# Down-projection of a two-layer diffusion backbone: the quarter sums re-signed and made by adding transfers

## The chip, the cores and the metric

The kernel runs on one core of one Trainium2 chip. The metric is the device time of one execution in microseconds (us); a shorter time is better. The engines are named as in the profile: PE is the matrix engine (PEld its weight loads), DVE the vector engine, ACT the scalar engine, POOL the GpSimd engine, SP the engine that issues most transfers (DMAs). An engine works through its own instructions in order and waits on semaphores for the others.

## The reference

Two layers, each with token mixing and a gated feed-forward part. The change is in the feed-forward part of the 1024 latent tokens; the rest is the same in both kernels.

```python
SEQ = 1024; D_MODEL = 1024; D_FF = 2816; DEPTH = 2

def conv_ffn(h, w_up, conv_w, conv_b, w_down):
    u = h @ w_up
    up = jnp.pad(u, ((0, 0), (1, 1), (0, 0)))
    u = up[:, :-2] * conv_w[0] + up[:, 1:-1] * conv_w[1] + up[:, 2:] * conv_w[2] + conv_b
    a, g = jnp.split(u, 2, axis=-1)
    return (a * jax.nn.silu(g)) @ w_down          # (1024 x 2816) @ (2816 x 1024)

# in each layer l, for the latent tokens x1 and the gate g2
ffn = conv_ffn(x1 * (1 + sc2) + sh2, w_up[l], conv_w[l], conv_b[l], w_down[l])
x = layer_norm(ALPHA * x1 + g2 * ffn, ln2_g[l], ln2_b[l])
```

## The kernel before, in words

All inputs are float32. A float32 product is made of three: each operand is split into a high part, a rounded copy that ACT makes (`whi`, line 1336 in the down-projection), and a low part, the rest, `source - high` (`wlo`, line 1337). `mm3` (lines 158 to 160) adds low*high, high*low and high*high into one PSUM bank, each matmul 128x128 by 128x512.

The down-projection multiplies the gated activations A (tokens by hidden channels) by the weights B (hidden by output channels). Both are cut into quarters, A11 to A22 and B11 to B22, and the product takes seven products of quarters in place of eight (Winograd's form). `DOWN` lists them in their order: P1 = A11 B11, P7 = S3 T3, P6 = S2 T2, P4 = A22 T4, P5 = S1 T1, P3 = S4 B22, P2 = A12 B21. S and T are sums and differences of quarters. A product runs over 11 blocks of 128 hidden channels for four tiles of 128 tokens: 11 x 4 x 3 = 132 matmuls. Its operands come in six steps of one block and then five times two; a step of two blocks is a transfer of 128x1024 floats, 512 KB, for either side.

Before the change every operand that is a sum is made on DVE by `tt` (line 1309) from one or two freshly loaded quarters, and two running sums are held in SBUF: X for the weights (T3, then T2 = T3 + B11) and Y for the activations (S3, then S2 = A22 - S3). T4, T1, S1 and S4 are made from X or Y and another load. DVE makes the low part of the activations, POOL that of the weights. All loads are issued by SP (lines 1292 and 1300). So each step of a product waits for its loads, for the sum, for the cast on ACT and for the low part.

`combine` (line 1354 for its adds) takes a product out of its four PSUM banks and adds it into p1, v and u; `post` (1369, 1370) multiplies by the gate and adds to the residual, which `load_resid` has loaded and scaled: `ga` on DVE (line 997) and `ba`, the beta, on POOL (line 998). These run while the next product is under way, a tile per step. The activations come from a scratch in DRAM, `act`, which the up-projection's `gate` writes (line 1242 is its last multiply) just ahead of the down-projection.

The order in which instructions stand on each engine is made when the kernel is built, by a scheduler that takes buffers and dependences into account; on each engine it is then fixed. The rings of buffers (`raw` for weights, two in each of two pools; `araw` for activations, three; high and low parts, three or four) bound how far the splits run ahead of the matmuls.

Of the kernel before, what the change touches and what calls it, by code (L numbers as in the profile page):

```python
# [19 lines left out]
P = 128  # L20
# [25 lines left out]
# how the parts of a layer's token mixing are laced, and which of their instructions go ahead of others  # L46
# [50 lines left out]
def hybrid_backbone_kernel(ctx: ExitStack, tc: tile.TileContext, A: dict, out: bass.AP):  # L97
# [13 lines left out]
    def f32(ap):  # L111
        return ap.bitcast(F32)

# [67 lines left out]
    def columns(pp, specs, eng=None):  # L181
        # parameter rows to one column per 128 of them
# [149 lines left out]
    # ================= token mixing: projections =================  # L332
# [15 lines left out]
    class Stages:  # L348
        # each use of a product runs its later stages after one and two further products
# [186 lines left out]
    # ================= attention =================  # L536
# [122 lines left out]
    # ================= Fourier mixing =================  # L659
# [85 lines left out]
    # ================= gated linear recurrence =================  # L745
    def recurrence(l, S, gp2, gp, psum):
# [57 lines left out]
        def pair_steps(i):  # L804
            # two tiles of tokens, 2 P of them, side by side
# [111 lines left out]
        # a pair of tiles starts when the one before is halfway  # L917
# [55 lines left out]
    # ================= residual update and layer norm =================  # L973
# [50 lines left out]
    # ================= output projection =================  # L1024
# [35 lines left out]
    # ================= gated convolutional feed-forward =================  # L1060
# [24 lines left out]
    def ffn_weights(fp, n, nraw):  # L1085
        # every fourth unit in a place of its own: one more than the common ring holds
# [11 lines left out]
    def conv(l, j, part, o, u):  # L1098
        # u has one token more than o on either side
# [29 lines left out]
    HALF = SEQ // 2  # L1129

# [44 lines left out]
    def up_early(l, j, h, rp, tag, parked):  # L1175
        # what the later tokens alone allow
# [45 lines left out]
    def up_all(l, fp, todo, ws, h, parked, act, bg):  # L1222
# [10 lines left out]
        def gate(j):  # L1233
            for t0 in (HALF, 0):
# [44 lines left out]
    NK = NJ // 2  # L1279
# [4 lines left out]
    def down_operands(l, f1, f2, f3, act):  # L1284
        X, Y = {}, {}
        count = [0, 0]

        def load_w(fw, q, ks):
            count[0] += 1
            t = (fw if count[0] % 2 else wp).tile([P, 1024], F32, tag="raw", bufs=2, name="raw")[:, 0:512 * len(ks)]  # L1290
            k0, c0 = NK * (int(q[1]) - 1) + ks[0], 512 * (int(q[2]) - 1)
            nc.sync.dma_start(out=t.rearrange("p (k c) -> p k c", c=512),
                              in_=A["w_down"][l, k0 * P:(k0 + len(ks)) * P, c0:c0 + 512].rearrange("(k p) c -> p k c", p=P))
            return t

        def load_a(q, ks, eng=None, first=False):
            t = (wp if first else f1[0]).tile([P, 1024], F32, tag="raw" if first else "araw", bufs=2 if first else 3,
                                              name="araw")[:, 0:512 * len(ks)]
            t0, k0 = HALF * (int(q[1]) - 1), NK * (int(q[2]) - 1) + ks[0]
            (eng or nc.sync).dma_start(out=t.rearrange("p (k c) -> p k c", c=512),  # L1300
                              in_=act[k0:k0 + len(ks), :, t0:t0 + HALF].rearrange("k p c -> p k c"))
            return t

        def hold(held, nm, n, size):
            held[n] = (f3[0] if nm == "X" else f2[0]).tile([P, size], F32, tag=f"{nm}{n}", bufs=1, name=nm)
            return held[n]
# [490 lines left out]
```

## Time and profile before

| what | value |
|---|---|
| time, median of three executions | 3447.15 us (3443.57 to 3452.46) |
| span of the profiled execution, first to last instruction | 3438.2 us |
| down-projection of layer 0 | from 1404.4 to 1688.6 us of the span |
| down-projection of layer 1 | from 3136.4 to 3420.6 us of the span |
| matmuls in one down-projection | 7 x 132 = 924 |

The profile gives the span of its own execution and no other total; the median lies 8.95 us above the span, which is taken as what stands around it. The two down-projections were found by the first and the last matmul into the banks `pd` of the latent tokens, and the seven products by every 132nd matmul. A wait is put down to the instruction that ended it; a busy engine counts only while it executes, so that a full window means an engine without a pause.

### The profile page before, as it was taken

Reading aid. Unit: us, or ns where it says so; the run is one execution under the profiler, and the core shown is the slowest. Engines: PE = TensorE matmul, PEld = TensorE weight load, DVE = VectorE, ACT = ScalarE, POOL = GpSimd, SP = SyncE. Lnnn points to the kernel's source line nnn. Section 1 sums busy time; section 2 is a strip of 40 time slices with the busy share of each in tenths; the row PEclk is TensorE's granted clock in tenths of the full one; section 3 lists DMA queues with packets and bytes.
Section 4 is the critical chain, followed back from the end, with each engine's and each line's share of the span. In section 5 each row is a group of like instructions: output and inputs, shape, how many; then the busy total and the mean of one; then the engine's idle time right before and its main releaser. Section 6 shows DMA issues by size and latency. Waiting matters only on the chain.

```text
span 3438.2 us, 55946 instructions
## 1 busy us (share of the span) xinstructions
PE 3118.6 (91%) x20897; PEld 2535.5 (74%) x20897; DVE 2545.4 (74%) x4167; ACT 1547.9 (45%) x3105; POOL 1412.7 (41%) x1138
## 2 busy tenths in 40 slices
PE   6999998989899999887899999998988889998885
PEld 4879976778666777666697888876766668776664
DVE  4614568877798887698766755668877798887888
ACT  4325556664443434333365435655642534444332
POOL 3521105422554444443435351115435645454545
PEclk9999999999999999999999999999989999999998
DMA  7643122127754443655675432122045532225643
GB/s 214 205 149 84 54 90 60 34 57 217 223 180 140 129 130 121 210 197 176 208 213 182 130 103 71 46 89 67 18 132 170 185 110 80 80 74 183 224 161 117
DMA packets 451396, 457.07 MB, mean 133 GB/s; under 512 B 31859, under 2 KB 343604, under 8 KB 451126
## 3 DMA queue, kind: packets, MB, share of 16 engines
q1 hardware_dynamic: 440342, 443.85, 40.9%
q0 software_dynamic: 10784, 9.66, 1.2%
q8 instruction: 165, 2.70, 0.3%
q14 instruction: 105, 0.86, 0.1%
HBM read 358.88 MB, written 94.54 MB: 132 GB/s over the span
## 4 chain that ended last, share of the span: by engine, by line
PE 17%; DVE 14%; issue 7%; POOL 6%; DMA 4%; ACT 2%; SPq 0%; POOLq 0%; DVEq 0%; ACTq 0%
POOL wlo L1216 3%; PE ps_t L602 2%; PE pu L159 2%; PE pu L158 2%; PE pu L160 2%; DVE cv L1105 1%; DVE wlo L1337 1%; PE ps_s L566 1%; DMA araw<-act 1%; PE ps_o L612 1%; PE ps_s L567 1%; PE ps_o L614 1%; PE pws L158 1%; PE pws L159 1%; PE pws L160 1%
## 5 line engine op out<-in xcount | busy, mean ns | idle before, releaser
L1216 POOL TENSOR_TENSOR wlo<-S,whi 128x512 fp32r<-128x512 f32 x176 | 282.5, 1615 | 279.3 <-ACT whi L1215 266.1
L1105 DVE SCALAR_TENSOR_TENSOR cv<-U,cw,cv 128x512 f32<-128x512 f32 x352 | 332.9, 994 | 32.5 <-ACT cv L1102 32.4
L158 PE MATMUL pd<-whi,wlo 128*128 128x512 f32 x616 | 251.4, 419 | 72.7 <-DVE wlo L1337 54.0
L569 DVE TENSOR_REDUCE mx<-ps_s 128x1 f32<-128x512 f32 (+1 forms) x400 | 222.2, 588 | 107.8 <-PE ps_s L567 106.5
L145 POOL TENSOR_TENSOR wlo<-raw,whi 128x1024 fp32r<-128x1024 f32 x69 | 167.4, 2429 | 300.6 <-ACT whi L144 300.6
L608 DVE TENSOR_TENSOR pl<-ps_t,ph 128x512 fp32r<-128x512 f32 x328 | 222.8, 685 | 85.2 <-ACT ph L607 83.0
L602 PE MATMUL ps_t<-ident,p 128*128 128x128 f32 x1312 | 261.9, 283 | 13.1 <-DVE pl L608 7.5
L159 PE MATMUL pd<-wlo,whi 128*128 128x512 f32 x616 | 255.6, 415 | 17.6 <-POOL wlo L1337 17.6
L576 ACT ACTIVATE p<-ps_s,mx 128x512 f32<-128x512 f32 (+1 forms) x400 | 242.7, 615 | 51.8 <-DVE mx L572 42.1
L607 ACT CAST ph<-ps_t 128x512 fp32r<-128x512 f32 x328 | 190.8, 589 | 160.8 <-PE ps_o L614 80.6
L160 PE MATMUL pd<-whi 128*128 128x512 f32 x616 | 252.0, 409 | 0.0
L1102 ACT ACTIVATE cv<-U,cb,cw 128x512 f32<-128x512 f32 x176 | 137.2, 812 | 254.3 <-DVE U L1231 209.6
L158 PE MATMUL pxs<-whi,hlo 128*128 128x256 f32 x752 | 221.6, 295 | 5.7 <-DVE hraw L1504 4.3
L1337 POOL TENSOR_TENSOR wlo<-raw,whi 128x1024 fp32r<-128x1024 f32 (+1 forms) x60 | 156.5, 2616 | 160.2 <-ACT whi L1336 151.0
L159 PE MATMUL pxs<-wlo,hhi 128*128 128x256 f32 x752 | 216.5, 288 | 0.5 <-DVE wlo L145 0.4
L160 PE MATMUL pxs<-whi,hhi 128*128 128x256 f32 x752 | 216.4, 288 | 0.0
L158 PEld LDWEIGHTS pd<-whi,wlo 128*128 128x128 f32 x616 | 122.0, 199 | 114.8 <-DVE wlo L1337 56.1
L612 PE MATMUL ps_o<-pl,V 128*128 128x256 f32 x656 | 200.4, 322 | 6.7 <-DVE pl L608 4.8
L1216 POOL TENSOR_TENSOR wlo<-raw,whi 128x512 fp32r<-128x512 f32 x108 | 149.9, 1395 | 128.0 <-ACT whi L1215 119.1
L556 POOL DMA_DIRECT2D qt<-QT x72 | 40.3, 560 | 373.9 <-PE ps_s L567 277.1
L602 PEld LDWEIGHTS ps_t<-ident,p 128*128 128x128 f32 x1312 | 164.2, 143 | 36.5 <-DVE pl L608 12.3
L1231 DVE TENSOR_TENSOR U<-pu,U 128x512 f32<-128x512 f32 x252 | 167.3, 685 | 25.5 <-PE pu L160 17.2
(395 smaller groups left out, 9680.2 us busy)
## 6 DMA issues: line engine op xcount, KB each, us to landing
raw<-in_w_up_dram SPq DMA_DIRECT2D x144, 512.0 KB
raw<-in_w_down_dram SPq DMA_DIRECT2D x102, 512.0 KB
raw<-in_w_ada_dram SPq DMA_DIRECT2D x96, 512.0 KB
araw<-act SPq DMA_DIRECT2D x80, 512.0 KB
act<-cv SPq DMA_DIRECT2D x88, 256.0 KB
raw<-in_w_in_dram SPq DMA_DIRECT2D x36, 512.0 KB
y<-r SPq DMA_DIRECT2D x28, 512.0 KB
r<-y SPq DMA_DIRECT2D x26, 512.0 KB
```

The source lines that it names most:

```text
L158: nc.tensor.matmul(o, lhsT=al, rhs=bh, start=start, stop=False)
L159: nc.tensor.matmul(o, lhsT=ah, rhs=bl, start=False, stop=False)
L160: nc.tensor.matmul(o, lhsT=ah, rhs=bh, start=False, stop=stop)
L569: nc.vector.tensor_reduce(out=mx[:, j:j + 1], in_=t[:, 0:n], axis=AX.X, op=ALU.max)
L576: nc.scalar.activation(out=t, in_=sc[j][:, 0:n], func=AF.Exp, bias=mx[:, 3:4], accum_out=su[:, h, j:j + 1])
L602: nc.tensor.transpose(t[:, ss, h, :], in_=ps2[h][2 * s2 + ss], identity=ident)
L607: nc.scalar.copy(ph, tv)
L608: nc.vector.tensor_tensor(out=pl, in0=tv, in1=f32(ph), op=ALU.subtract)
L612: nc.tensor.matmul(o, lhsT=V[:, s, kv, 1:3, :].rearrange("p a c -> p (a c)"), rhs=pl[:, ss, :], start=(s == 0), stop=False)
L1105: nc.vector.scalar_tensor_tensor(out=o, in0=u[:, tap:tap + n], scalar=convw[l][tap][:, c:c + 1], in1=o, op0=ALU.mult, op1=ALU.add)
L1216: nc.gpsimd.tensor_tensor(out=lo, in0=src, in1=f32(hi), op=ALU.subtract)
L1337: eng.tensor_tensor(out=lo, in0=src, in1=f32(hi), op=ALU.subtract)
```

## The change

A sum in SBUF can be made by a transfer that adds what it brings to what is there. Such a transfer only adds, so the signs are moved: half of the activations are stored negated in the scratch (the gate's last multiply gets a factor of -1 for the later tokens of the lower hidden channels and the earlier tokens of the upper ones), and the adds and subtractions in `combine` and `post` are changed to match. Every S and T is now a plain sum.

- `hold` loads the first quarter of X and of Y for every step during P1 (SP), and an adding transfer issued by POOL brings the second.
- `next_sum` adds the next quarter to X and Y after the operand's split, during P7 and P6. P4's T4 and P3's S4 are then X and Y as they stand; before, each was a load and a subtraction.
- S1 and T1, for P5, are each a plain load and an adding transfer into the same buffer.
- No sum of quarters is left on DVE. The low parts of the weights move from POOL to DVE, and so does the beta of the residuals of this stage.

Per down-projection and counted in sets of six steps (eleven blocks, 2.88 MB), there were 16 sets of plain loads; now there are 10 of plain loads and 8 of adding ones.

```diff
-                nc.vector.tensor_tensor(out=cv[1], in0=cv[1], in1=cv[0], op=ALU.mult)
+                if (j < NK) == (t0 > 0):
+                    nc.vector.scalar_tensor_tensor(out=cv[1], in0=cv[1], scalar=-1.0, in1=cv[0], op0=ALU.mult, op1=ALU.mult)
+                else:
+                    nc.vector.tensor_tensor(out=cv[1], in0=cv[1], in1=cv[0], op=ALU.mult)
...
-        def tt(o, x, y, op=ALU.subtract, eng=nc.vector):
-            eng.tensor_tensor(out=o, in0=x, in1=y, op=op)
-            return o
+        def plus(t, part):
+            nc.gpsimd.dma_start(out=halves(t), in_=part, accum_op=ALU.add)
+            return t
+
+        def hold(n, ks):
+            for held, pl, nm, part, x, y in ((X, f3[0], "X", w_part, "B22", "B12"), (Y, f2[0], "Y", a_part, "A11", "A21")):
+                held[n] = pl.tile([P, 512 * len(ks)], F32, tag=f"{nm}{n}", bufs=1, name=nm)
+                nc.sync.dma_start(out=halves(held[n]), in_=part(x, ks))
+                plus(held[n], part(y, ks))
...
-            if q == "S3":
-                x, y = load_a("A11", ks), load_a("A21", ks)
-                return tt(hold(Y, "Y", n, 512 * len(ks)), x, y)
-            if q == "S2":
-                return tt(Y[n], load_a("A22", ks), Y[n])
-            t = load_a("A11" if q == "S1" else "A12", ks)
-            return tt(t, t, Y[n], ALU.add if q == "S1" else ALU.subtract)
+            return plus(load_a("A22", ks), a_part("A21", ks)) if q == "S1" else Y[n]
...
-            if q == "T3":
-                x, y = load_w(fw, "B22", ks), load_w(fw, "B12", ks)
-                return tt(hold(X, "X", n, 512 * len(ks)), x, y)
-            if q == "T2":
-                return tt(X[n], X[n], load_w(fw, "B11", ks), ALU.add)
-            t = load_w(fw, "B21" if q == "T4" else "B22", ks)
-            return tt(t, X[n], t) if q == "T4" else tt(t, t, X[n])
+            return plus(load_w(fw, "B11", ks), w_part("B12", ks)) if q == "T1" else X[n]
+
+        def next_sum(q, n, ks):
+            if q in ("S3", "S2"):
+                plus(Y[n], a_part("A22" if q == "S3" else "A12", ks))
+            if q in ("T3", "T2"):
+                plus(X[n], w_part("B11" if q == "T3" else "B21", ks))
...
-            return split(fw if own else wp, "x" if own else "", 1 if own else 3, side_b(fw, q, n, ks), nc.gpsimd)
+            r = split(fw if own else wp, "x" if own else "", 1 if own else 3, side_b(fw, q, n, ks), nc.vector)
+            next_sum(q, n, ks)
+            return r
...
-            rs[i] = load_resid(fp, y1[i], ga, ba, 6, after=after, engs=(nc.vector, nc.gpsimd))
+            rs[i] = load_resid(fp, y1[i], ga, ba, 6, after=after, engs=(nc.vector, nc.vector))
...
                 w = split_w(qb, n, ks)
+                if p == "P1":
+                    hold(n, ks)
```

The scheduler places the new instructions; two places matter. On SP, at the start of layer 0's P1, the transfers stood like this (`raw` of weights and `araw` of activations, the first `araw` rows of P1, then `ga`, `ba`, `g2` and `r` of the residual, and P7's loads behind):

```order
L1292 DMA raw_15582<-in_w_down_dram 128x2x512
L1300 DMA araw_15442<-act0_11747 128x2x512
L1300 DMA araw_15492<-act0_11747 128x2x512
L1300 DMA araw_15534<-act0_11747 128x2x512
L1292 DMA raw_15540<-in_w_down_dram 128x2x512
L1243 DMA act0_11747<-cv0_15343 128x512
L1300 DMA araw_15576<-act0_11747 128x2x512
L1243 DMA act0_11747<-cv0_15354 128x512
L1300 DMA araw_15622<-act0_11747 128x512
```

and now stand like this:

```order
L1309 DMA raw_15612<-in_w_down_dram 128x2x512
L1326 DMA X_15400<-in_w_down_dram 128x512
L1326 DMA Y_15403<-act0_11747 128x512
L1326 DMA X_15424<-in_w_down_dram 128x2x512
L1326 DMA Y_15427<-act0_11747 128x2x512
L1315 DMA araw_15454<-act0_11747 128x2x512
L1247 DMA act0_11747<-cv0_15343 128x512
L1247 DMA act0_11747<-cv0_15354 128x512
L1326 DMA X_15466<-in_w_down_dram 128x2x512
L1326 DMA Y_15469<-act0_11747 128x2x512
L976 DMA ga_15472<-in_ln1_g_dram 128x1024
L976 DMA ba_15475<-in_ln1_b_dram 128x1024
```

Before, all loads of P1 stood ahead of or between the last two stores of `act`. Now the loads of X and Y stand between them, and of P1's activations only those of step 2 (`araw_15454`) come before the stores; those of steps 3 to 5 and the weights of step 4 stand behind.

On DVE, at the end of the same product, the order was this (`araw_15534` and `araw_15576` are the activations of P1's steps 4 and 5, `Y_15626` the sum for P7's step 0, `r` the residual):

```order
L1337 TENSOR_TENSOR wlo_15537<-araw_15534,whi_15536 128x1024
L1309 TENSOR_TENSOR Y_15626<-araw_15622,araw_15624 128x512
L1337 TENSOR_TENSOR wlo_15579<-araw_15576,whi_15578 128x1024
L997 TENSOR_TENSOR r_15462<-r_15462,ga_15454 128x1024
L997 TENSOR_TENSOR r_15504<-r_15504,ga_15454 128x1024
L1337 TENSOR_TENSOR wlo_15629<-Y_15626,whi_15628 128x512
```

and is now this (`raw_15564` and `raw_15612` are the weights of P1's steps 4 and 5, `araw_15606` the activations of its step 5, `X_15424` and `X_15400` P7's steps 1 and 0):

```order
L1348 TENSOR_TENSOR wlo_15561<-araw_15558,whi_15560 128x1024
L1348 TENSOR_TENSOR wlo_15687<-X_15424,whi_15686 128x1024
L1348 TENSOR_TENSOR wlo_15567<-raw_15564,whi_15566 128x1024
L1348 TENSOR_TENSOR wlo_15615<-raw_15612,whi_15614 128x1024
L1348 TENSOR_TENSOR wlo_15664<-X_15400,whi_15663 128x512
L997 TENSOR_TENSOR r_15576<-r_15576,ga_15472 128x1024
L998 TENSOR_TENSOR r_15576<-r_15576,ba_15475 128x1024
L1348 TENSOR_TENSOR wlo_15609<-araw_15606,whi_15608 128x1024
```

Low parts of X, which P7 takes and which an adding transfer completes, now stand ahead of the low parts of P1's last two steps.

## Rows read from the trace of the kernel before

**Rows 1.** The page: engines over the span, transfer queues.
```profile
PE 3118.6 (91%) x20897; PEld 2535.5 (74%) x20897; DVE 2545.4 (74%) x4167; ACT 1547.9 (45%) x3105; POOL 1412.7 (41%) x1138
...
q1 hardware_dynamic: 440342, 443.85, 40.9%
q0 software_dynamic: 10784, 9.66, 1.2%
```

**Rows 2.** Layer 0 by product, in the order P1 to P2: engines, clock, transfers.
```profile
core 0: us, PE busy (x) PEld busy (x) DVE busy (x) ACT busy (x) POOL busy (x), PEclk, DMA share, GB/s
1404.40:1445.30 40.90, 31.69 (x132) 24.43 (x133) 29.20 (x21) 13.33 (x20) 22.64 (x9) 0.98 0.72 253
1445.30:1489.00 43.70, 36.38 (x132) 27.33 (x133) 32.46 (x21) 15.26 (x18) 18.52 (x8) 0.87 0.77 268
1489.00:1525.40 36.40, 31.77 (x133) 24.36 (x131) 36.40 (x23) 14.61 (x16) 23.30 (x9) 1.00 0.45 154
1525.40:1559.80 34.40, 33.41 (x133) 25.75 (x134) 31.16 (x28) 9.14 (x10) 15.48 (x6) 0.95 0.49 168
1559.80:1598.40 38.60, 34.05 (x134) 26.67 (x133) 33.71 (x42) 12.37 (x16) 14.40 (x5) 0.91 0.54 178
1598.40:1646.40 48.00, 34.53 (x133) 26.86 (x132) 39.61 (x49) 18.37 (x27) 23.48 (x16) 0.86 0.62 205
1646.40:1688.60 42.20, 36.57 (x166) 29.43 (x165) 32.36 (x35) 10.62 (x14) 18.88 (x9) 0.96 0.54 164
```

**Rows 3.** Layer 1: P7, P6 and P2, and the sum over seven products.
```profile
3178.80:3217.70 38.90, 34.79 (x133) 26.38 (x134) 30.93 (x21) 15.42 (x18) 18.46 (x8) 0.89 0.85 300
3217.70:3254.00 36.30, 31.11 (x133) 24.34 (x131) 36.30 (x23) 14.68 (x16) 23.40 (x9) 0.98 0.47 157
...
3371.10:3420.60 49.50, 35.74 (x133) 27.21 (x132) 47.13 (x50) 8.54 (x10) 27.49 (x15) 0.86 0.31 105
sum 284.20, PE 235.44 PEld 182.01 DVE 244.56 ACT 88.78 POOL 154.08; mean PE 33.63 PEld 26.00 DVE 34.94 ACT 12.68 POOL 22.01
```

**Rows 4.** A stretch of P4 of layer 0, tile pd alone.
```profile
1532.00:1550.00 18.00, 17.73 (x76) 13.64 (x75) 4.66 (x8) 0.00 (x0) 1.00 0.44 147
```

**Rows 5.** What PE waited for: total us, times, longest; layer 0, then layer 1.
```profile
PE pd L158 <- DVE wlo L1337: 22.3, 8, 9.4
PE pd L159 <- POOL wlo L1337: 9.6, 9, 2.9
PE pd L158 <- ACT whi L1336: 9.1, 4, 6.3
...
PE pd L158 <- DVE wlo L1337: 31.8, 14, 8.6
PE pd L158 <- ACT whi L1336: 9.6, 3, 7.7
```

**Rows 6.** Instructions by line and shape, layer 0's stage: busy us, mean ns | idle.
```profile
L1309 DVE TENSOR_TENSOR raw<-X,raw 128x1024 f32<-128x1024 f32 x5 | 13.6, 2756 | 0.8 <-DMA raw<-in_w_down_dram 0.8
...
L1309 DVE TENSOR_TENSOR raw<-raw,X 128x1024 f32<-128x1024 f32 x5 | 6.0, 1215 | 0.0
...
L1337 POOL TENSOR_TENSOR wlo<-raw,whi 128x1024 fp32r<-128x1024 f32 x24 | 65.7, 2743 | 58.0 <-ACT whi L1336 54.5 <-DVE p L1369 3.4
```

**Rows 7.** Line 1309 alone over both stages, then line 1337 alone.
```profile
sum 568.40, DVE 164.56; mean DVE 82.28
...
sum 568.40, DVE 126.73 POOL 213.61; mean DVE 63.36 POOL 106.81
```

**Rows 8.** Transfers that POOL issues, line 556: ns, and us to landing.
```profile
L556 POOL DMA_DIRECT2D qt<-QT x72: 527/549/643, 280.0 to 2462.9; - x72
...
DMA to landing us min/median/max: 2.3/2.5/6.4
```

**Rows 9.** SP in order of time, layer 0's P1: start, us, line.
```profile
1400.68 1.65 SPq L1300 DMA_DIRECT2D araw<-act  x3
...
1416.22 0.33 SPq L1243 DMA_DIRECT2D act<-cv  x1
```

**Rows 10.** Lines 1242 and 1105, all instances: ns min/median/max.
```profile
L1242 DVE TENSOR_TENSOR cv<-cv,cv x88: 674/679/1781, 971.2 to 3148.1; 128x512 f32<-128x512 f32 x88
...
L1105 DVE SCALAR_TENSOR_TENSOR cv<-U,cw,cv x352: 734/746/2864, 965.5 to 3142.0; 128x512 f32<-128x512 f32 x176
```

More of the change, by code (lines that the diff above doesn't have):

```diff
@@ L1129, in hybrid_backbone_kernel @@
     HALF = SEQ // 2
+    NK = NJ // 2
     def h_pair(hp, nm):
@@ L1273, in up_all @@
         return lambda: gate(NJ - 1)
-    NK = NJ // 2
     DOWN = (("P1", "A11", "B11"), ("P7", "S3", "T3"), ("P6", "S2", "T2"), ("P4", "A22", "T4"), ("P5", "S1", "T1"),
@@ L1286, in down_operands, with w_part, a_part, halves @@
         count = [0, 0]
+        def w_part(q, ks):
+            k0, c0 = NK * (int(q[1]) - 1) + ks[0], 512 * (int(q[2]) - 1)
+            return A["w_down"][l, k0 * P:(k0 + len(ks)) * P, c0:c0 + 512].rearrange("(k p) c -> p k c", p=P)
+        def a_part(q, ks):
+            t0, k0 = HALF * (int(q[1]) - 1), NK * (int(q[2]) - 1) + ks[0]
+            return act[k0:k0 + len(ks), :, t0:t0 + HALF].rearrange("k p c -> p k c")
+        def halves(t):
+            return t.rearrange("p (k c) -> p k c", c=512)
         def load_w(fw, q, ks):
@@ L1290, in load_w @@
             t = (fw if count[0] % 2 else wp).tile([P, 1024], F32, tag="raw", bufs=2, name="raw")[:, 0:512 * len(ks)]
-            k0, c0 = NK * (int(q[1]) - 1) + ks[0], 512 * (int(q[2]) - 1)
-            nc.sync.dma_start(out=t.rearrange("p (k c) -> p k c", c=512),
-                              in_=A["w_down"][l, k0 * P:(k0 + len(ks)) * P, c0:c0 + 512].rearrange("(k p) c -> p k c", p=P))
+            nc.sync.dma_start(out=halves(t), in_=w_part(q, ks))
             return t
@@ L1298, in load_a @@
                                               name="araw")[:, 0:512 * len(ks)]
-            t0, k0 = HALF * (int(q[1]) - 1), NK * (int(q[2]) - 1) + ks[0]
-            (eng or nc.sync).dma_start(out=t.rearrange("p (k c) -> p k c", c=512),
-                              in_=act[k0:k0 + len(ks), :, t0:t0 + HALF].rearrange("k p c -> p k c"))
-            return t
-        def hold(held, nm, n, size):
-            held[n] = (f3[0] if nm == "X" else f2[0]).tile([P, size], F32, tag=f"{nm}{n}", bufs=1, name=nm)
-            return held[n]
-        def tt(o, x, y, op=ALU.subtract, eng=nc.vector):
-            eng.tensor_tensor(out=o, in0=x, in1=y, op=op)
-            return o
+            (eng or nc.sync).dma_start(out=halves(t), in_=a_part(q, ks))
+            return t
+        def plus(t, part):
[6 more added lines that the diff above has]
+                plus(held[n], part(y, ks))
         def side_a(q, n, ks, first):
@@ L1342, in split_w, with split_a @@
             own = count[1] % 4 == 0
-            return split(fw if own else wp, "x" if own else "", 1 if own else 3, side_b(fw, q, n, ks), nc.gpsimd)
-        return (lambda q, n, ks, first=False: split(wp if first else f1[0], "" if first else "a", 3,
-                                                     side_a(q, n, ks, first), nc.vector)), (lambda fw: lambda *q: split_w(fw, *q))
+            r = split(fw if own else wp, "x" if own else "", 1 if own else 3, side_b(fw, q, n, ks), nc.vector)
+            next_sum(q, n, ks)
+            return r
+        def split_a(q, n, ks, first=False):
+            r = split(wp if first else f1[0], "" if first else "a", 3, side_a(q, n, ks, first), nc.vector)
+            next_sum(q, n, ks)
+            return r
+        return split_a, (lambda fw: lambda *q: split_w(fw, *q)), hold
     def down_all(l, fp, fa, ops, ready, y1, rows, finish, deferred, halfway):
-        split_a, split_w = ops
+        split_a, split_w, hold = ops
         p1, v, u = ([fa.tile([P, 512], F32, name=f"{t}{m}") for m in range(4)] for t in ("p1", "v", "u"))
@@ L1369, in post @@
                     eng.tensor_tensor(out=o, in0=c, in1=rows()[2][:, sl], op=ALU.mult)
-                    eng.tensor_tensor(out=rs[i][:, sl], in0=rs[i][:, sl], in1=o, op=ALU.add)
+                    eng.tensor_tensor(out=rs[i][:, sl], in0=rs[i][:, sl], in1=o, op=ALU.subtract if direct else ALU.add)
         def stats(i, half):
@@ L1388, in combine @@
             elif p == "P6":
-                add(u[m], c, p1[m])
-                add(v[m], c, v[m])
+                add(u[m], c, p1[m], ALU.subtract)
+                add(v[m], c, v[m], ALU.subtract)
             elif p == "P4":
                 t = fp.tile([P, 512], F32, tag="tmp", bufs=2, name="tmp")
-                add(t, v[m], c, ALU.subtract)
+                add(t, c, v[m], ALU.subtract)
                 post(later, (t,), nc.vector)
@@ L1396, in combine @@
             elif p == "P5":
-                add(v[m], c, v[m])
-                add(u[m], c, u[m])
+                add(v[m], v[m], c, ALU.subtract)
+                add(u[m], u[m], c, ALU.subtract)
                 post(later, (None, v[m]), nc.vector)
@@ L1402, in combine @@
             elif p == "P3":
-                add(u[m], c, u[m])
+                add(u[m], u[m], c, ALU.subtract)
             else:
@@ L1755, in halfway @@
                         pass
-            down_all(l, fp, f2[0], (ops[0], ops[1](fw)), ready, y1, lambda: rows(0), finish, deferred, halfway)
+            down_all(l, fp, f2[0], (ops[0], ops[1](fw), ops[2]), ready, y1, lambda: rows(0), finish, deferred, halfway)
             acs.close()
```

## The prediction, made before the result was known

> **What bounds the kernel now.** I read the page first: PE is busy 91% of the span, so time is gained only where PE stands still [rows 1]. Then the two down-projections by product: both take 284.2 us for 924 matmuls [rows 2, 3]. PE's pace without a wait comes from a stretch at full clock: 76 matmuls in 18.0 us [rows 4], 0.237 us each, 31.3 us for a product and 219 us for seven. So 65 us of each stage are not matmul pace, 130 us in both: the most this change can return, unless it shortens something outside.
>
> Who takes the 65 us is seen in DVE's column. In P6 DVE is busy 36.40 of 36.40 us in layer 0 and 36.30 of 36.30 in layer 1 [rows 2, 3]: the product is exactly as long as DVE's work. P3 has 39.6 of 48.0, layer 1's P2 47.1 of 49.5. PE's own waits agree: of those above, 54.1 us end with a low part on DVE, 9.6 in layer 0 with one on POOL, and 18.7 with ACT's cast [rows 5]; the casts wait in turn for a sum or a load. P1 and P7 are different: DVE is busy for 62 of 85 us, while the transfers run at a share of 0.72 to 0.85 and up to 300 GB/s [rows 2, 3]. These two products wait for data.
>
> DVE's work is also stretched. The same subtraction of 128x1024 floats takes 1215 ns for T1 and 2756 ns for T4 [rows 6]; T4's are made during P6, where POOL is busy for 23.3 of 36.4 us [rows 2]. I take the stretch for DVE and POOL reading operands at the same time. Line 1309 has 48 such sums per stage, 164.6 us in both [rows 7]; 40 of full size at 1.215 and eight of half size would be 53 us per stage, not 82.
>
> **What goes.** The 48 sums: 82 us of DVE per stage [rows 7]. The weights' low parts on POOL: 107 us per stage [rows 7], and its beta. **What comes on DVE**: 42 low parts of weights and 8 betas, at 1.215 us for 43 full ones and half of that for 7 halves, 57 us. Taking contention out saves more: DVE's own 42 low parts cost 63 us per stage and would cost 46. DVE falls from 240 us per stage (234.9 summed from rows 2, 244.6 in rows 3) to about 240 - 82 + 57 - 17 = 198, and less where other two-input operations were stretched. POOL keeps adding transfers and small operations; an issue costs 0.55 us at 128 KB [rows 8], and 48 of them, taken at twice that for the larger ones, 53 us. POOL is no bound by its work.
>
> Product by product: P6 loses 30 us of sums and gains 7 us of low parts, so it falls to PE's pace. I put P6 and P4 at 32.5 us each, P5 at 33; before they were 36.4, 34.4 and 38.6. P3 and P2 keep adds, residuals, normalisation and transposes: 36 and 37 from 48.0 and 42.2 in layer 0. These five fall from 199.6 to 171, by 28 us. In layer 1 P2 keeps POOL's scaling of finished tiles beside DVE (POOL 27.5 us there [rows 3]), so I leave it 43 of its 49.5; from 202.9 (284.2 less 81.3 for P1 and P7) to 177, by 26.
>
> **What the transfers cost.** A plain 512 KB load at full share: 300 GB/s at 0.85 is 353 GB/s [rows 3], 1.49 us. No adding transfer stands in this trace. Lower bound: it costs what POOL's plain queue costs. q0 moved 9.66 MB in 1.2% of the span, 234 GB/s; q1 443.85 MB in 40.9%, 316 GB/s [rows 1]. So 1.35 times, 2.0 us. Upper bound: 128 KB land in 2.5 us at the median [rows 8]; four of those one after another are 10 us. I take 3.0 us, near the queue's own rate: an add in place reads two and writes one where a copy reads one and writes one, 1.5 times the accesses. Per stage that is 10 plain sets of 5.5 x 1.49 us, 82; 8 adding sets of 5.5 x 3.0, 132; some 16 other full-size transfers (residuals, rows, results), 24. Together 238 us of transfers, under 284 but above 219: no cover is left if adds are dearer.
>
> **Where it gets worse: P1.** SP issued three loads of `araw` from 1400.7 and waited for DVE's gate until the last store of `act` at 1416.2 [rows 9]. In the new order the loads of P1's steps 3 to 5 stand behind that store, among the loads of X and Y; sixteen plain transfers up to step 5's activations. 16 x 1.49 is 24 us, and about four adding ones beside them 12: 1452. With cast, low part and two blocks of matmuls (8 us) P1 ends near 1460, 15 us later than now. DVE also holds P1's last splits behind two splits of X, so a late add delays P1 itself. P7 then finds most sums made and runs at 31.3 us, to 1491: 2 us later than the 1489.0 of now. In layer 1 P7 is 4.8 us shorter before, so I count 6. P7's and P6's next sums, 12 x 3.0 = 36 us each, are issued up to three steps ahead of PE and cover P6 and P4 just so.
>
> The rest is priced at nothing. The gate's factor turns 44 multiplies of 679 ns into the form that takes 746 ns in line 1105 [rows 10]: 3 us of DVE in all, hidden by matmuls, 3 us if not. The bank adds only change sign. The same ring lengths remain, so no split runs further ahead than before.
>
> Sum: -28 + 2 and -26 + 6 are -46 us. From the profiled execution's span that is 3392; the median of the runs stands 8.95 us above the span, so 3401 us.
>
> **A rule of the Trainium skill.** No run here shows what an add costs in the transfer engines. The Trainium skill, Collectives: The Full Stack, Part 3, says that a reducing transfer needs two source reads on the same read ring and so runs at half the rate of a copy. By that rule the add would be 2 x 2.0 = 4.0 us, and the sum would come to the second case below.
>
> **The rivals.**
> (a) Forecast, 0.40: adds at 2.5 to 3.5 us, 3401, by itself 3380 to 3425.
> (b) Adds at 4.0 us, the two reads alone deciding, twice a plain transfer of q0, 0.16. P1 ends 6 us later still, near 1466, P7 at 1497. The sixteen adds still open at 1458 take 64 us, to 1522; P6's twelve 48 more, to 1570, when P4 should have ended at 1561; then twelve for P5, to 1618, leave P3 and P2 to end at 1686. Stage gain 3 us: 3441. Against it: queue q0's row, which is far below that price; for it: nothing in the trace shows an add's second read for free. The Trainium skill's page on collectives, named above, is the one that speaks for this case.
> (c) Slower, 0.25: adds above 4.2 us. At 6 us the 44 full-size adds fill 264 us and the rest 106; transfers set the stage, 370 us where it was 284: +86 twice, 3619. At 5 us it is 326, 3531; at the upper bound, 10 us, 546 and 3971. It decides from the price at which 44 adds and 106 us exceed 284, 4.05 us. It would be felt in P1 to P6, where six of the eight sets lie. For it: P1 and P7 already run the transfers at 0.72 to 0.85. Against: P4 to P2 run them at 0.31 to 0.62, so half of the stage has room.
> (d) Adds near the lower bound, 2.0 us, 0.15: P1 ends at 1456, P7 at 1487, DVE never waits: -54, 3393, and 3383 if P2 of layer 1 too comes down to 33 us.
> (e) DVE isn't relieved as I think, since its queue stands still on late adds or keeps its stretched durations, 0.04: the gain of P6 to P2 halves, the loss in P1 stays: 3428.
>
> **Numbers.** A measurement of this kernel tells about 0.3%, 10 us, from no change. Faster by more: (a), (d), (e) and a third of (b), less some of their tails: 0.62. Same: 0.13, mostly (b). Slower: (c), 0.25. The range runs from 3360, below (d), to 3540, which holds (c) up to an add of about 5 us; left out is some 0.07 below and 0.13 above.
>
> **What would show it.** Right: no DVE sum of quarters in the stage; low parts on DVE near 1.22 us; P6 at about 32 us with DVE idle in it; adding transfers landing within some 4 us of their issue; P1 longer by 10 to 20 us and P7 near 31. Wrong: casts or DVE's low parts that wait for transfers in P6 to P5; a transfer share near 1 with a rate below 250 GB/s, the sign that adds cost more than 4 us; POOL standing on an add whose predecessor hasn't landed while SP's loads pass it; a P6 still as long as DVE's work.

## The result and the profile after

The changed kernel takes 3407.18 us (median of 4 runs, 3404.24 to 3419.26); the kernel before took 3445.36 us on the same chip. The ratio is 0.9897, with a 95% interval of 0.9878 to 0.9915: faster by 1.0%, where 46 us or 1.3% were forecast, and 6 us above the 3401 us of the prediction. The profiled execution is the longest of the four, 3419.26 us, so its stages may be up to 12 us long in all. One execution of run e3 below took 3743.65 us at a granted clock of 0.76, where its other five took 3365.58 to 3375.16 us; e3's ratio leaves it out.

The page of the changed kernel answers to [rows 1]. PE does the same matmuls; DVE is relieved, 34.61 MB have left SP's queue q1, and 46.14 MB have come to POOL's q0: two sets more in each stage, 11.53 MB, are moved than before.

```profile
PE 3116.8 (91%) x20897; PEld 2540.3 (74%) x20897; DVE 2417.0 (71%) x4171; ACT 1550.2 (45%) x3105; POOL 1261.6 (37%) x1134
...
q1 hardware_dynamic: 422294, 409.24, 37.9%
q0 software_dynamic: 34848, 55.80, 8.6%
```

Layer 0 by product, P1 to P2, with the sum, in the columns of [rows 2]:

```profile
1408.70:1470.90 62.20, 39.24 (x132) 29.45 (x133) 27.48 (x29) 18.40 (x25) 16.67 (x16) 0.78 1.00 281
1470.90:1501.70 30.80, 30.80 (x133) 24.78 (x132) 17.22 (x17) 11.86 (x14) 14.64 (x13) 1.00 1.11 248
1501.70:1532.50 30.80, 30.80 (x133) 24.78 (x132) 12.98 (x13) 10.41 (x11) 13.72 (x13) 1.00 1.13 210
1532.50:1563.90 31.40, 31.15 (x134) 24.66 (x133) 21.20 (x31) 10.85 (x13) 4.45 (x4) 1.00 1.04 238
1563.90:1607.40 43.50, 35.05 (x133) 27.43 (x132) 26.43 (x39) 13.86 (x19) 5.96 (x5) 0.88 0.90 232
1607.40:1641.80 34.40, 31.82 (x133) 24.54 (x132) 31.68 (x47) 17.49 (x24) 5.10 (x8) 1.00 0.52 177
1641.80:1678.50 36.70, 35.13 (x165) 27.69 (x163) 34.40 (x49) 12.43 (x16) 2.12 (x5) 1.00 0.72 221
sum 269.80, PE 233.98 PEld 183.33 DVE 171.39 ACT 95.29 POOL 62.66; mean PE 33.43 PEld 26.19 DVE 24.48 ACT 13.61 POOL 8.95
```

Layer 1: P1, P5 and the sum, to be held against [rows 3].

```profile
3132.30:3198.00 65.70, 39.14 (x132) 29.45 (x133) 28.14 (x30) 18.48 (x25) 16.71 (x15) 0.74 1.05 297
...
3288.70:3324.50 35.80, 31.19 (x133) 24.47 (x132) 26.63 (x34) 13.14 (x15) 5.10 (x5) 1.00 1.00 267
...
sum 264.60, PE 225.59 PEld 178.24 DVE 170.49 ACT 87.65 POOL 72.85; mean PE 32.23 PEld 25.46 DVE 24.36 ACT 12.52 POOL 10.41
```

The two stages, 284.2 us each before [rows 2, 3], are 269.8 and 264.6 us: 34.0 us of gain. P7, P6 and P4 are now bare matmul pace, and DVE is idle in more than half of P6, where it was full before. What eats into the gain is in the first row of each layer: P1 has grown from 40.9 to 62.2 us in layer 0, and the transfers' share, the column before the last, is 1.00 to 1.13 from P1 to P4, with the clock granted in P1 down to 0.78. PE itself is busy 7.6 us longer there for the same matmuls, 39.24 us against 31.69 at a clock of 0.98 [rows 2]; the rest is waiting. The bound moved from DVE to the transfers, which e3 tests below.

PE's waits by kind (total us, times, longest; layer 0, then layer 1) answer to [rows 5]. The low part that PE waits longest for is in P1 now.

```profile
PE pd L158 <- DVE wlo L1348: 24.5, 7, 12.4
PE pd L158 <- ACT whi L1347: 4.6, 3, 2.1
...
PE pd L158 <- DVE wlo L1348: 25.7, 7, 13.1
```

Why that low part is late shows in the order of time in layer 0's P1 (start, us, what it waited for). DVE stands 18.3 us on the first residual row, which is loaded among the X and Y of `hold`. But the low part behind it could hardly have come sooner: SP issued the load of its activations at 1420.06, ACT's cast of them waited for that load until 1442.45, and the low part waited for the cast.

```profile
1420.06 0.37 SPq L1315 DMA_DIRECT2D araw<-act  x1
...
1440.32 1.23 DVE L997 TENSOR_TENSOR r<-r,ga 128x1024 f32<-128x1024 f32 x1 [18.29 <-DMA r<-y]
...
1442.45 1.05 ACT L1347 CAST whi<-araw 128x1024 fp32r<-128x1024 f32 x1 [6.51 <-DMA araw<-act]
...
1443.53 1.23 DVE L1348 TENSOR_TENSOR wlo<-araw,whi 128x1024 fp32r<-128x1024 f32 x1 [0.65 <-ACT whi L1347]
```

A low part on DVE by shape (busy us, mean ns), against the 1215 and 2756 ns of the sums in [rows 6]: no kind of DVE's 128x1024 work of this stage is stretched any more.

```profile
L1348 DVE TENSOR_TENSOR wlo<-raw,whi 128x1024 fp32r<-128x1024 f32 x20 | 24.2, 1218 | 0.3 <-ACT whi L1347 0.3
```

The adding transfers of line 1319, all instances of one kind (ns min/median/max of the issue on POOL), and the landing of all, answer to [rows 8]:

```profile
L1319 POOL DMA_DIRECT2D X<-in_w_down_dram x36: 884/1195/3099, 1412.0 to 3252.5; - x36
...
DMA to landing us min/median/max: 5.6/15.9/25.0
```

### The profile page after: what moved, and what is told of

The parts are those of the page before. It is cut to its first block, busy times and chain, and to the rows that moved or that the text cites. A ratio compares the mean times of both kernels' runs of the same rounds, so it can differ in the third digit from the quotient of the medians.

```text
span 3417.4 us, 55716 instructions
## 1 busy us (share of the span) xinstructions
PE 3116.8 (91%) x20897; PEld 2540.3 (74%) x20897; DVE 2417.0 (71%) x4171; ACT 1550.2 (45%) x3105; POOL 1261.6 (37%) x1134
## 3 DMA queue, kind: packets, MB, share of 16 engines
q0 software_dynamic: 34848, 55.80, 8.6%
## 4 chain that ended last, share of the span: by engine, by line
PE 28%; DVE 16%; DMA 14%; issue 9%; POOL 9%; ACT 3%; SPq 0%; POOLq 0%; DVEq 0%; ACTq 0%
PE pu L158 4%; POOL wlo L1217 4%; PE pu L159 4%; PE pu L160 4%; DMA araw<-act 3%; DMA X<-in_w_down_dram 3%; DVE cv L1105 3%; DMA raw<-in_w_down_dram 2%; PE ps_t L602 2%; PE ps_s L566 1%; DVE wlo L1348 1%; PE ps_o L612 1%; DVE U L1232 1%; DMA hraw<-yT 1%; DVE S L1204 1%
## 5 line engine op out<-in xcount | busy, mean ns | idle before, releaser
L1217 POOL TENSOR_TENSOR wlo<-S,whi 128x512 fp32r<-128x512 f32 x176 | 283.0, 1618 | 281.9 <-ACT whi L1216 268.2
L1105 DVE SCALAR_TENSOR_TENSOR cv<-U,cw,cv 128x512 f32<-128x512 f32 x352 | 326.0, 974 | 33.9 <-ACT cv L1102 33.8
L602 PE MATMUL ps_t<-ident,p 128*128 128x128 f32 x1312 | 263.1, 284 | 13.6 <-DVE pl L608 8.1
L160 PE MATMUL pxs<-whi,hhi 128*128 128x256 f32 x752 | 216.4, 288 | 0.0
L614 PE MATMUL ps_o<-ph,V 128*128 128x256 f32 x656 | 183.2, 297 | 0.0
```

Source lines behind the costliest of these rows:

```text
L160: nc.tensor.matmul(o, lhsT=ah, rhs=bh, start=False, stop=stop)
L602: nc.tensor.transpose(t[:, ss, h, :], in_=ps2[h][2 * s2 + ss], identity=ident)
L1105: nc.vector.scalar_tensor_tensor(out=o, in0=u[:, tap:tap + n], scalar=convw[l][tap][:, c:c + 1], in1=o, op0=ALU.mult, op1=ALU.add)
L1217: nc.gpsimd.tensor_tensor(out=lo, in0=src, in1=f32(hi), op=ALU.subtract)
```

## The experiments

All ratios are to the kernel before, run beside each on the same chip (its medians were 3446.88 to 3448.76 us), with 95% intervals. Lengths of products are from the first matmul of one to that of the next in the profiled execution, as in [rows 2]; "P1 to P6" is P1, P7 and P6 together.

| run | sums | low parts, betas | median us | ratio | interval |
|---|---|---|---|---|---|
| e1 | DVE | DVE, DVE | 3374.36 | 0.9789 | 0.9770 to 0.9807 |
| e2 | adds | POOL, DVE | 3446.97 | 0.9999 | 0.9986 to 1.0012 |
| e3 | left out, plain transfers in their place | DVE, DVE | 3371.67 | 0.9775 | 0.9756 to 0.9795 |
| e4 | adds; later tiles' residual loads in P6 | DVE, DVE | 3405.48 | 0.9881 | 0.9863 to 0.9899 |
| e5 | DVE | DVE, POOL | 3387.99 | 0.9819 | 0.9798 to 0.9839 |
| e6 | T2, S2, T4, S4 adds, rest DVE | DVE, DVE | 3402.98 | 0.9863 | 0.9843 to 0.9883 |
| e7 | S4 adds, rest DVE | DVE, DVE | 3363.86 | 0.9752 | 0.9729 to 0.9775 |
| e8 | DVE; residual loads in P6 | DVE, DVE | 3367.90 | 0.9763 | 0.9743 to 0.9784 |
| e9 | DVE; spare work on POOL | DVE, DVE | 3455.02 | 1.0026 | 1.0014 to 1.0039 |
| e10 | as e6, T3 and S3 made in P7 | DVE, DVE | 3409.53 | 0.9893 | 0.9873 to 0.9913 |
| e11 | e7 and e8 together | DVE, DVE | 3354.63 | 0.9734 | 0.9715 to 0.9754 |
| e12 | e11, T4 adds too | DVE, DVE | 3374.42 | 0.9782 | 0.9757 to 0.9807 |

**Which part gains.** e1 is the kernel before with two words changed: the engine of the weights' low parts and that of the beta. e2 is the changed kernel with the first of them taken back.

```
e1, from before:  -  side_b(fw, q, n, ks), nc.gpsimd)          + ..., nc.vector)
                  -  engs=(nc.vector, nc.gpsimd))              + engs=(nc.vector, nc.vector))
e2, from after:   -  side_b(fw, q, n, ks), nc.vector)          + ..., nc.gpsimd)
```

> The kernel before with one half of the change alone: the low parts of the weights and the stage's beta go from POOL to DVE, the sums of quarters stay on DVE. Theory (the gain of the change comes from taking the sums off DVE; DVE is the bound of P6 to P2): DVE gets 57 us more per stage and loses its stretch, 240 + 57 - 17 - 29 = 251 us of 284, so P6 stays at DVE's pace and the time stays within 15 us of before: 3435 to 3460. Rival (a quiet POOL alone is the gain, since DVE's operations then take 1.22 us): P6 to P2 fall as in the changed kernel and P1 stays short, 3385 to 3405.

> The changed kernel with the low parts of the weights back on POOL; adding transfers and the beta on DVE stay. Theory (sums off DVE are the gain, and POOL must be free to issue the adds in time): DVE is relieved still, but POOL's queue holds 107 us of low parts per stage between its adds, each add waits for those ahead of it, and PE waits for low parts on POOL in P7 to P4: 15 to 60 us slower than the changed kernel, 3420 to 3465. Rival (who makes the low parts does not matter once the sums are off DVE): within 10 us of the changed kernel, 3397 to 3417.

e1 gains 2.1%, twice what the whole change gains, with all 48 sums still on DVE: its theory fell, and it lies 11 us under even its rival's range. e2, which has no sums on DVE, gains nothing. P6 and P5 of e1 and its sum over layer 0:

```profile
1480.70:1511.50 30.80, 30.80 (x134) 24.78 (x133) 30.19 (x31) 12.51 (x13) 0.00 (x0) 1.00 0.64 215
...
1542.30:1573.10 30.80, 30.80 (x134) 24.78 (x133) 30.16 (x46) 12.63 (x17) 0.00 (x0) 1.00 0.60 192
...
sum 238.90, PE 225.79 PEld 177.66 DVE 216.36 ACT 93.20 POOL 3.93; mean PE 32.26 PEld 25.38 DVE 30.91 ACT 13.31 POOL 0.56
```

DVE is busy for 30.2 of 30.8 us in P6, but PE does not wait for it: P6 to P5 run at matmul pace. DVE's whole stage is 216 us, less than PE's 219 at pace, although it holds the sums and all low parts. The sums themselves, line 1309, are 52.9 us in layer 0, 84.2 before, with POOL's column at zero; one kind of them (ns min/median/max) that [rows 6] has at a mean of 2756:

```profile
L1309 DVE TENSOR_TENSOR raw<-X,raw x6: 683/1216/1218, 1501.8 to 1522.3; 128x1024 f32<-128x1024 f32 x5, 128x512 f32<-128x512 f32 x1
...
sum 238.90, DVE 52.89; mean DVE 52.89
```

In e2 POOL makes the low parts beside the adds, and DVE's own low parts go back from 1.22 us to 2.12. Its time is in its theory's range, but not by the waits that the theory named: P7, P6 and P4 of layer 0 are at pace, 30.8 us each, and the loss is in P1 and P5, 69.5 and 50.1 us.

```profile
L1348 POOL TENSOR_TENSOR wlo<-X,whi 128x1024 fp32r<-128x1024 f32 x15 | 46.2, 3271 | 4.2 <-ACT whi L1347 4.2
...
L1348 DVE TENSOR_TENSOR wlo<-Y,whi 128x1024 fp32r<-128x1024 f32 x15 | 31.8, 2121 | 22.7 <-ACT whi L1347 22.6
```

So the four corners are 3449 (neither), 3374 (low parts and betas alone), 3447 (adds, with low parts on POOL) and 3407 us (both): on top of the move to DVE the adds lose 33 us.

**What an add costs.** e3 makes the adding transfers plain ones: same bytes, same queue, same order. The second operand of each sum then replaces the first one, so the sums are left out.

```
-            nc.gpsimd.dma_start(out=halves(t), in_=part, accum_op=ALU.add)
+            nc.gpsimd.dma_start(out=halves(t), in_=part)
```

> The changed kernel with every adding transfer made a plain one on the same queue with the same waits; the second quarters overwrite the first, so the sums are left out. Theory (an add keeps the transfer engines busy twice as long as a plain transfer, and they are full from P1 to P5): 512 KB take some 1.6 us in place of 2.8, the transfers of P1 end about 6 x 1.2 + queue = 8 to 12 us sooner, P5 loses its waits: 20 to 40 us faster than the changed kernel, 3367 to 3387. Rival (the order of the queues and the latency of a dependent transfer make P1 and P5 late, not the price of an add): P1 stays above 58 us, time within 10 us of the changed kernel.

By the medians it is 35 us faster than the changed kernel, as its theory said. Its page has for the queues:

```profile
q1 hardware_dynamic: 422294, 409.24, 38.5%
q0 software_dynamic: 23584, 55.80, 5.1%
```

The same 55.80 MB take q0 8.6% of 3417.4 us with adds, 293.9 us, and 5.1% of 3371.5 us plain, 171.9. Of both 41 us are the 9.66 MB that were there before [rows 1]. Left for the equivalent of 88 transfers of 512 KB are 253 and 131 us: 2.87 us an add, 1.49 us a plain transfer. One thing more differs: the plain transfers move in packets of 4 KB, the adds in packets of 2 KB, hence the two counts of packets. That is not the price. In the changed kernel's own trace a 2 KB packet of an add takes 178 ns on average, one of the plain transfers on q1 95.5. Nor is it that the engines are full: e11's adds, where they are not, take 189 ns a packet. In the first products of layer 0 the price is seen in the rate: e3's P7 has a share of 1.03 at 378 GB/s, the changed kernel's 1.11 at 248.

```profile
1410.30:1462.20 51.90, 38.69 (x133) 28.85 (x134) 27.55 (x29) 18.64 (x25) 11.61 (x17) 0.84 0.98 360
1462.20:1493.00 30.80, 30.80 (x134) 24.78 (x133) 17.39 (x17) 11.67 (x14) 10.90 (x16) 1.00 1.03 378
```

P1 is 51.9 us even so: of its growth from 40.9 to 62.2 us half stays when the transfers are plain and the other half goes with the adding. P5 is back at 30.8 us.

**Is it POOL's work beside DVE's?** Two runs give POOL less and more of it. e5 leaves the eight betas of a stage there; e9 gives e1's POOL subtractions that nobody uses.

```
e5, from e1:  -  engs=(nc.vector, nc.vector))     + engs=(nc.vector, nc.gpsimd))
e9, from e1:  +  spare = u[3] if p in ("P1", "P7", "P6") else p1[0]
              +  for kk in range(len(ks)):
              +      hi = f32(w[0][:, kk, :])
              +      nc.gpsimd.tensor_tensor(out=spare, in0=hi, in1=hi, op=ALU.subtract)
```

> The kernel before, with one edit: the low parts of the weights of the down-projection are made on DVE instead of POOL; the betas of the residual stay on POOL, the sums stay on DVE. Theory (POOL's long subtractions slow DVE's own work; the eight betas that are left on POOL are short beside them): most of the gain of the run with low parts and betas on DVE, 3369 to 3382 us. Rival (what counts is that POOL reads nothing at all, the betas too, or that the residual's path is shorter): 3390 us or more.

> The kernel before with low parts and betas on DVE, and POOL given subtractions that nobody uses: for each 128x512 of weights in the down-projection it subtracts the rounded part from itself into a tile that is free at the time, 77 a stage. Theory (POOL's reading slows DVE): DVE's 128x1024 subtractions, 1.13 us with a quiet POOL, stretch to 1.5 us or more, and most of the gain is lost: 3420 to 3475 us. Rival (what was slow before were the waits of TensorE and of the buffers for POOL's results, and these are gone): DVE stays at 1.13 us, 3372 to 3388 us.

e5 fell between its two expectations: 13.6 us above e1 by the medians, with intervals that just overlap. POOL works for 24.3 us in layer 0's stage, 3.05 us for each beta:

```profile
L998 POOL TENSOR_TENSOR r<-r,ba 128x1024 f32<-128x1024 f32 x8 | 24.3, 3047 | 80.5 <-PE pd L159 49.9 <-DVE r L997 25.8 <-issue 4.8
```

e9 gives back all of e1's gain and a little more, 81 us, though the kernel needs nothing of what POOL makes. (In P4 the first spare subtraction overwrites `p1[0]` before P6's combination has read it, so one block of tokens takes it in place of P1's product.) In layer 0, whose stage is 38.8 us longer than e1's, no instruction waits for these subtractions; in layer 1 three casts on ACT do, 11.3 us in all. The rival, that what was slow before were the waits for POOL's results, is out. POOL's two kinds of spare work; layer 0's sum; and the sums that e1 makes in 1.22 us at most (the 1.13 us of the expectation is a mean that takes in the 128x512 ones):

```profile
L1424 POOL TENSOR_TENSOR p<-whi 128x512 f32<-128x512 f32 x44 | 67.0, 1523 | 57.3 <-ACT whi L1336 36.9 <-DVE r L1370 12.7 <-DVE u L1354 5.2
L1424 POOL TENSOR_TENSOR u<-whi 128x512 f32<-128x512 f32 x33 | 54.7, 1658 | 85.1 <-ACT whi L1336 83.5
...
sum 277.70, PE 239.02 PEld 184.32 DVE 261.51 ACT 93.94 POOL 126.90; mean PE 34.15 PEld 26.33 DVE 37.36 ACT 13.42 POOL 18.13
...
L1309 DVE TENSOR_TENSOR raw<-X,raw x6: 678/1211/2058, 1516.7 to 1541.8; 128x1024 f32<-128x1024 f32 x5, 128x512 f32<-128x512 f32 x1
```

DVE's busy time in the stage goes from 216.4 to 261.5 us with the same instructions. The three ways to load POOL agree on a price, layer 0's stage taken for both: 24.3 us a stage cost 13.6 us in the kernel's time, 121.7 cost 80.7, and the 129.1 of before (106.4 of low parts in layer 0, 22.7 of betas) cost 74.4, so 0.28 to 0.33 us of the whole for each us of POOL in the two stages.

**Where the adds hurt.** e4 takes the residual that DVE stands on out of P1. e6 and e10 make half of the sets on DVE again; in e6 T3 and S3 are still made in P1, in e10 in P7 as before.

```
e4, from after:  -  PLAN = [(("P1", m + 2), load_r, ...        + PLAN = [(("P6", m + 2), load_r, ...
e6, from after:  hold():     -  plus(held[n], part(y, ks))
                             +  t = load_w(fw, y, ks) if nm == "X" else load_a(y, ks)
                             +  nc.vector.tensor_tensor(out=held[n], in0=held[n], in1=t, op=ALU.add)
                 S1, T1:     two loads and a tensor_tensor on nc.vector in place of a load and plus()
e10, from e6:    the body of hold() is done by side_a and side_b when P7 asks for S3 and T3
```

> The changed kernel with the four residual loads of the later tiles, and with them ga, ba and g2, moved from P1 to P6. Theory (transfers fill P1; and DVE stood 18 us on the first residual, SP on its buffer): seven transfers of 1.5 us leave P1, 10 us per stage, and the waits in the queues with them; P1 falls from 62 and 66 us to 45 to 52, P6 gets them but has PE work to hide them: 15 to 30 us faster than the changed kernel, 3377 to 3392. Rival (the bytes are only moved, the transfers stay full until P5 and the same time is lost later): within 8 us of the changed kernel.

> The changed kernel, with four of its eight sets of sums made on DVE again from two loads each (T3 and S3 in P1, T1 and S1 in P5); only T2, S2, T4 and S4 are made by adding transfers. Theory (each set of adding transfers costs time because the transfers are full): between the run with low parts and betas on DVE alone (3374 us) and the changed kernel (3407 us), 3375 to 3390 us, with P1 shorter than 55 us and P5 near 31. Rival (the adds behind P7 and P6 are the dear ones, or any adds hold up the first products as much): 3395 to 3410 us.

> The changed kernel with T3 and S3 made on DVE in P7, when P7 takes them, in place of in P1, and T1 and S1 on DVE in P5; T2, S2, T4 and S4 by adding transfers as in the changed kernel. Theory (the loss is P1's, which carries the operands of P7 beside its own): P1 near 39 us and P7 36 to 40, 3360 to 3378 us. Rival (the adds that are issued in P7 and P6 cost as much wherever T3 and S3 are made): 3390 to 3405 us, with P7 or P6 longer by what P1 gains.

All three end with the changed kernel, 3405, 3403 and 3410 us, and their theories fell. Each shortens the product that it is aimed at and lengthens another; only P5 is the better for having T1 and S1 on DVE, 31 to 33 us in e6 and e10. P1 to P6 take 123.8 and 126.1 us in the two layers of the changed kernel, 121 and 122 in e4, 124 and 128 in e6, 124 and 135 in e10, against 104.5 and 105.2 in e1 and 113.5 and 114.8 in e3. The place of T3 and S3 is not what costs, nor their adds; the adds for T2, S2, T4 and S4, common to all four, are what is left, issued while the operands of P1 and P7 are loaded. That they are the cause follows from what is ruled out; the changed kernel without these four sets alone was not run. The new signs are ruled out too, since e7 and e11 below have them. In e10 one sees how. P7 and P6 of layer 0, then three kinds of waits in P7 (total us, times, longest):

```profile
1447.00:1500.00 53.00, 35.96 (x133) 26.84 (x133) 23.97 (x22) 13.08 (x15) 16.53 (x15) 0.84 1.09 288
1500.00:1530.80 30.80, 30.80 (x133) 24.78 (x132) 19.01 (x22) 11.13 (x12) 8.50 (x7) 1.00 1.11 236
```

```profile
ACT whi L1360 <- DVE Y L1327: 19.3, 4, 8.0
...
DVE Y L1327 <- DMA araw<-act: 11.8, 4, 5.4
DVE X L1327 <- DMA raw<-in_w_down_dram: 10.8, 4, 4.4
```

The cast waits for a sum, the sum for a plain load, and that load shares full transfers (1.09) with adds for P6, which nobody needs before P7 is over. That the plain loads would be served first if the adds were issued later was not tried.

**One set where there is room.** e7 keeps one set of adds, S4, issued in P4 and P5; e8 is e1 with e4's edit; e11 joins them; e12 adds T4, issued in P6.

```
e7, from e1, re-signed:  def next_sum(q, n, ks):
                             if q == "S1":
                                 plus(Y[n], a_part("A12", ks))
e12, from e11:               if q == "T2":
                                 plus(X[n], w_part("B21", ks))
                         and T1 from two loads
```

> The re-signed kernel with low parts and betas on DVE, all sums on DVE except one set: S4, which P3 takes, is made by adding transfers behind P5's sums, where the transfers have room. Theory (DVE is the bound of P3 in the run with low parts and betas on DVE, 38 and 44 us, and an add where the transfers have room is free): P3 near 34 us, 3360 to 3372 us. Rival (P3 waits for something else, or the adds delay P3's loads by as much): no gain over 3374 us, 3370 to 3382 us.

> The kernel before with low parts and betas on DVE, and the loads of the residual of the later tiles moved from P1 to P6. Theory (DVE in P1 stands on the first residual, behind which the low parts of P1 and P7 are queued): P1 and P7 shorter by 3 to 7 us in each layer, 3360 to 3370 us. Rival (the bytes only move, as in the changed kernel with the same edit): 3370 to 3378 us.

> The re-signed kernel with all sums on DVE except S4, made by adding transfers (3363.9 us), and the loads of the residual of the later tiles moved from P1 to P6 (3374 to 3368 us where that was tried without the adds). Theory (the two act in different products, P3 and P7, and add up): 3352 to 3361 us. Rival (P3 is where DVE's backlog ends, and the residual's work moved to P6 lengthens it there): 3361 to 3368 us.

> As the run with S4 by adds and late residual loads, and T4 too is made by adding transfers, issued in P6; T1 is then made from two loads in P5. Theory (eight fewer sums on DVE in P4, so less of a backlog in P3): 3 to 8 us under the run without it, 3346 to 3357 us. Rival (the transfers of P6 have no room, P4 waits for its adds): 3 to 10 us above the run without it, P4 over 33 us.

e7 and e8 land as their theories said, 3363.9 and 3367.9 us, though their intervals still touch e1's; e11, whose interval is clear of it, adds them up to 3354.6. P7 is at pace in e8 and e11, 30.8 and 30.3 us, where e1 has 35.4 and 36.6: without adds in these products the late residual does help, which it did not among them (e4). P3 of layer 1 in e8, then in e11:

```profile
3261.70:3306.00 44.30, 34.73 (x134) 27.16 (x133) 40.79 (x51) 16.95 (x22) 16.61 (x16) 0.88 0.50 170
```

```profile
3256.90:3293.60 36.70, 32.90 (x133) 25.68 (x132) 32.10 (x45) 16.42 (x22) 16.87 (x16) 0.95 0.42 138
```

The sums are off DVE's list there, and an add lands in 7.6 us at the median in e11, where the changed kernel needs 15.9. Layer 0's P3 gains nothing from e8 to e11 (40.3 and 40.7 us); there ACT's casts queue behind others that wait 2.4 to 2.7 us for DVE's work on the next layer's input, and why this varies from run to run I leave open. e12 fell: it loses 20 us, with executions spread from 3358 to 3380, and P4, which its rival had named as the loser, is at 30.8; P6 itself, in which the adds are issued, grows from 30.8 to

```profile
1479.70:1514.90 35.20, 31.80 (x134) 24.64 (x133) 28.96 (x29) 11.71 (x16) 4.75 (x4) 1.00 0.87 242
```

in layer 0 and from 31.1 to 39.3 in layer 1. P5, whose T1 now needs two loads, grows as well, from 31.7 to 34.7 and from 30.1 to 36.7 us. In P6 of layer 0 DVE stands 6.2 us on a residual row and casts wait 12.6 us for X; which of this makes the loss is open. e11 beats the kernel before by 2.7% and the changed kernel by some 52 us, with 12 of the changed kernel's 96 adds kept.

## Why the prediction was right, and where it was not

**What bounds the kernel: right.** DVE, stretched by POOL, set P6 to P2, and of "I take the stretch for DVE and POOL reading operands at the same time" e9 now shows that POOL's work stretches DVE's; no run tells its reading from its writing. The Trainium skill, SBUF — State Buffer, section Who interferes with whom, says that a DVE instruction with two inputs in SBUF contends with a GpSimd instruction that reads SBUF, not with one that only writes it. The runs agree as far as they go: 1.22 us for a 128x1024 sum with POOL quiet, a mean of 2.76 us for T4 beside POOL's subtractions of 2.74 [rows 6], up to 2.06 us beside e9's of 1.5 to 1.7.

**"What goes: the 48 sums": the step that failed.** The forecast gave the gain to the sums' departure and priced the low parts' arrival as a cost of 57 us and the contention at 17 us. It is the other way round. In e1 DVE keeps the sums and takes the 57 us, 240 + 57 = 297 us by the prediction's numbers, and measures 216: contention was worth some 80 us of DVE's time a stage, 30 of them in the sums themselves and the rest in low parts, residuals and combinations. In the changed kernel DVE is at 171 us, not at 198. The prediction did see 53 us under the 82 of the sums, but let those 29 us count for the sums' departure; it never asked what DVE would be with the sums kept and POOL quiet. By its own terms that is 240 - 29 - 17 + 57 = 251 us, too much for PE's 219; measured it is just under, 216 and 219 us in the two layers. The mis-sized term is the contention, and with it the adds looked needed.

**Product by product.** P6, P4 and P7: right, 30.8, 31.4 and 30.8 us where 32.5, 32.5 and 31.3 stood; so were P3 and P2 of layer 0 (34.4, 36.7 for 36, 37). Layer 1's P2, left at 43 us for POOL's scaling, is 35.6. P5 is wrong: 43.5 and 35.8 us for 33. P6 was to lose 30 us of sums on DVE; line 1309 has 26.8 there. The gain from P6 to P2 is 22.8 us in layer 0 (28 forecast) and 34.3 in layer 1 (26).

**The price of an add: right.** 3.0 us taken, 2.87 measured, and 1.49 for a plain one as taken. The rule of the Trainium skill named in the prediction, two source reads and half the rate (Collectives: The Full Stack, Part 3, where it is told of ReduceScatter), agrees by its ratio: 2.87 by 1.49 is 1.93. I had applied it to q0's average of 2.0 us, which is a rate of short transfers; from the plain price in the full stretch it would have given 2.98 us, the forecast's own number. Rivals (b), (c) and (d) fall with that, and (e) with DVE's 171 us. (The sum of (b) is 5 us short by its own terms: 1618 + 36 + 37 is 1691, so it stood for no gain.)

**What the price does: wrong in size.** P1 was to be 15 us longer and is 21.3 and 23.3; P1 and P7 together lose 8.4 and 14.7 us where I had 2 and 6. An add was to land within some 4 us and needs 15.9: the sum of 238 us of transfers under 284 was an average over the stage, and the load isn't spread like that. From P1 to P4 the share is 1.00 or more, in P3 and P2 it is 0.52 and 0.72. The sign named for it, a share near 1 below 250 GB/s, is there in P7 to P4, but at 2.87 us an add and not at the 4 us of which it was to tell; casts do wait for transfers in P5. Also missed was what DVE does in P1: it stands 18.3 us on a residual row that has nothing to do with the product. That cost little, since the activations behind it landed no sooner, and e4, which takes the residual away, gains nothing in all.

**The sum.** -28 + 2 - 26 + 6 = -46 us was forecast; -22.8 + 8.4 - 34.3 + 14.7 = -34.0 us is in the profiled stages. Against the forecast P6, P4, P3 and P2 came out 16 us better over the two layers, P5 13 us worse, P1 and P7 15 us worse. Of the 34.0 us the two profiled spans show 20.8: 4.3 us are lost ahead of layer 0's stage, 6.0 between the two and 2.9 behind the second, for which the forecast had 3 us at most and of which no run shows the cause. Nor do the 8.95 us by which the median stood above the span stand around it: where a run gives both, span and time differ by about 2 us, so the execution profiled before was some 7 us quicker than the median, and the one profiled after 12 us slower. That the time came out near is luck in part. Split by the runs, the move of the low parts and betas alone gains 74 us where the prediction's own terms gave it next to nothing, and the adds, which were to bring the gain, lose some 33.

## What to carry to other kernels

When two engines slow each other, first move the work that disturbs, alone, and measure again: two words gave twice the gain of the whole rewrite. Moving work from a full engine into transfers paid here for one set in eight, where the transfers had room; where they were full it lost, and T4's adds lost even in P6, whose share without them is 0.62. So read the share product by product, not over the stage, and add one move at a time. And a forecast can be right in time with its parts wrong, so run each half of a change by itself.

## What the runs showed of the hardware

- An accumulating transfer into SBUF costs 2.87 us of all transfer engines per 512 KB, a plain one on the same queue 1.49. Its issue takes 1.2 us of POOL at the median; landing takes 7.6 us in e11 and 15.9 in the changed kernel, whose transfers are full from P1 to P4.
- POOL's elementwise work beside DVE's costs about 0.3 us of this kernel's time for each us that POOL is busy, whether anyone uses the result or not.
- The issues of the adds occupy POOL too (55.4 us in layer 0's stage of the changed kernel), but DVE's low parts stay at 1.22 us beside them: POOL's elementwise work disturbs, its issuing of transfers does not.
